# Seven products in place of eight in the second MLP layer of a streaming encoder, with the sums of weights on GpSimd

## The chip, the core and the metric

The kernel runs on one core of one Trainium2 chip. The metric is the device time of one execution in microseconds (us), lower is better. The engines are TensorE (PE, with its weight loads as PEld), VectorE (DVE), ScalarE (ACT), GpSimd (POOL) and SyncE (SP), which here issues all transfers.

## The reference, cut to what matters

One layer of a streaming encoder: a retention and convolution mixer, then an MLP with residuals and norms. The change lies in the MLP, for 2192 tokens, width 1024, inner width 4096, in float32:

```python
h = rms_norm(x, g_pre_mlp)
f = jnp.square(jax.nn.relu(h @ w_mlp_in)) @ w_mlp_out
x = x + rms_norm(f, g_post_mlp)
```

## The kernel before

**Precision.** Every float32 operand is split into a high part (a copy to the format fp32r, on ScalarE) and a low part (operand minus high part, on GpSimd: the residue). A product of two operands is three matmuls: high x high, high x low, low x high.

**Tiling.** Tokens are in six groups; the MLP takes them in three pairs (`FG`, index `G`), one after the other. The tokens of a pair are cut in two column halves `c` of 384, 384 and 320 columns (`NH2`). The inner width is walked in 16 blocks `b` of two 128-row tiles (`FB = 2`). For each block layer 1 makes four tiles (two rows by two column halves); layer 2 of the block before multiplies them by a 256 x 1024 slice of the second weight matrix and adds the result into eight output tiles for each half, `ya`, in SBUF.

**Layer 1** is done in seven products P1 to P7 in place of eight (a Strassen-Winograd scheme over two halves of the input width, two weight tiles and two column halves). Each product is 12 matmuls. Products accumulate in three PSUM banks `mm`; the partial sums are read out and combined by ScalarE and VectorE (`copy`, `added`), squared relu is taken in `out`, and `split` makes high and low parts `fh`, `fl`. In the first pair the sums of first-layer weights are made on GpSimd in `fetch_product` and kept in DRAM (`wprod`); the second and third pair load them.

**Layer 2** (`l2_tile`): for each output tile (`q`, `o`) and half `c` six matmuls go into one PSUM bank (`cv` or `aux` in turn) and one VectorE addition takes it into `ya`: 16 tiles in a block. Its weights come as four raw loads of 512 columns in a block; each is copied to the high part by ScalarE and gets its residue from GpSimd (`split_unit`).

**Order.** `plan` writes out the steps: after each product of layer 1 in block `b` come two or three tiles of layer 2 of block `b - 1`. `next_unit` fetches weights ahead, up to `WB - 2` = 7 slots out of `WB` = 9. Between the steps `tick` advances generators: in the first and the second pair, from block 2 on, `prologue` prepares the next pair (norms, residual, differences; it uses PSUM banks of `aux` as `pacc` and `sw`, additions and differences on GpSimd, and loads on SyncE's queue). The program order gives priorities; a planner with estimated costs fixes the final order on each engine before the run, so instructions of both layers are interleaved, and each engine then runs its own list in order.

Of the kernel before, what the change touches and what calls it, by code (L numbers as in the profile page):

```python
# [12 lines left out]
F32 = mybir.dt.float32  # L13
F32R = mybir.dt.float32r
# [67 lines left out]
P1, P2, P3, P4, P5, P6, P7 = range(7)  # L82
ORDER = (P1, P2, P6, P5, P7, P3, P4)
NG = 3
NH2 = [384, 384, 320]


def plan():


    for G in range(NG):
        for b in range(NFB):
            steps = []
# [3 lines left out]
            done = 0  # L97
            for n, x in enumerate(ORDER):
# [53 lines left out]
def build(nc, T):  # L152
    lg = _log_gamma()
    with tile.TileContext(nc, schedule_with_timeline_sim=True) as tc, ExitStack() as top:
# [6 lines left out]
        catp = ep(tc.tile_pool(name="catp", bufs=1))  # L161
        yop = ep(tc.tile_pool(name="yop", bufs=2))
        np_ = ep(tc.tile_pool(name="np_", bufs=2))
# [48 lines left out]
        for G, b, steps in plan():  # L212
            for what, x in steps:
                if what == "p":
                    units.append(("p", G, (b, x)))
                elif what == "w":
                    units.append(("l2", G, x))
        WB = 9
        rawps, RB = [], [5]
# [9 lines left out]
        def fetch(i):  # L229
# [10 lines left out]
            if kind == "p":  # L240
                return fetch_product(i, *units[i])
            hi = wpool.tile([P, 1024], F32R, tag="w", name="whi", bufs=WB)
            lo = wpool.tile([P, 1024], F32R, tag="w", name="wlo", bufs=WB)
# [25 lines left out]
        def fetch_product(i, _, G, bx):  # L269
# [31 lines left out]
            if NG > 1:  # L301
                keeping[i] = (wprod[b, x], op, None)

        unit_i = [0]

        def next_unit(kind, g, f):
# [846 lines left out]
        def layer1(G, b):  # L1153

            n = NH2[G]
            fh = [fp.tile([P, FB, NM], F32R, tag=f"fh{c}", name=f"fh{c}") for c in range(2)]
            fl = [fp.tile([P, FB, NM], F32R, tag=f"fl{c}", name=f"fl{c}") for c in range(2)]
            banks = {}
# [24 lines left out]
            def added(ps, t):  # L1183
                r = yop.tile([P, NM], F32, tag="yo", name="c", bufs=3)[:, :n]
                nc.vector.tensor_tensor(out=r, in0=ps, in1=t, op=ALU.add)
                return r

            def out(i, c, src, r=None):

                if r is None:  # L1190
                    r = yop.tile([P, NM], F32, tag="yo", name="r", bufs=3)[:, :n]
                    nc.scalar.activation(out=r, in_=src, func=AF.Relu)
                    nc.vector.scalar_tensor_tensor(out=r, in0=src, scalar=0.0, in1=r, op0=ALU.max, op1=ALU.mult)
                else:
                    nc.scalar.activation(out=r, in_=r, func=AF.Relu)
                    nc.scalar.activation(out=r, in_=r, func=AF.Square)
                split(r, fh[c][:, i, :n], fl[c][:, i, :n])

            def run():
                s1 = copy(product(P1, "y", True))  # L1200
                yield
                r = added(product(P2, "z", True), s1)
                out(0, 0, None, r)
                yield
# [5 lines left out]
                r = added(banks["w"], u3)  # L1210
                out(1, 1, None, r)
# [4 lines left out]
                out(1, 0, product(P4, "y", False))  # L1216
                yield

            return (fh, fl), run()

        def l2_tile(G, b, c, q, o, w, fhl, ya):
            whi, wlo = w
            fh, fl = fhl
            n = NH2[G]
            ps = mm_bank()[:, :n]
            mm3(ps, (lambda k: whi[:, (k * NO + o) * P:(k * NO + o + 1) * P],
                     lambda k: wlo[:, (k * NO + o) * P:(k * NO + o + 1) * P]),
                lambda k: fh[c][:, k, :n], lambda k: fl[c][:, k, :n], FB)
            y = ytile(ya, c, q * NO + o, n)
# [19 lines left out]
        def last_layer2(G, w, fhls, ya):  # L1249
# [5 lines left out]
            for c in range(2):  # L1255
                acc = np_.tile([P, WM], F32, tag="acc", name="acc")[:, :n]
                accs = [acc, st_tile()[:, :n]] if c else [acc]
                for q in range(FB):
                    for o in range(NO):
# [5 lines left out]
                                 lambda i: cols(w[i // FB * FB + q][1], i % FB)),  # L1265
                            lambda i: fhls[i // FB][0][c][:, i % FB, :n], lambda i: fhls[i // FB][1][c][:, i % FB, :n],
                            2 * FB)
# [21 lines left out]
        for G, b, steps in plan():  # L1289
# [7 lines left out]
            cur, run = layer1(G, b)  # L1297
            w = {}
            for what, x in steps:
# [3 lines left out]
                elif what == "w":  # L1303
                    w[x] = next_unit("l2", G, x)
                else:
                    q, o, c = x
# [70 lines left out]
```

## Time and profile before

| | |
|---|---|
| median of 3 runs | 2451.93 us (2447.64 to 2454.78) |
| profiled execution, its own time | 2451.31 us |
| its span, first to last instruction | 2449.4 us |
| TensorE busy | 2358.0 us (96%) |
| VectorE busy | 1512.6 us (62%) |
| ScalarE busy | 913.3 us (37%) |
| GpSimd busy | 1135.8 us (46%) |

The MLP's first pair runs from about 957 us to 1460 us, the second to about 1960 us, the third to the end. A busy share of TensorE counts overlapping matmuls once; how fast it works is read from the distance between the starts of matmuls.

### The profile page before, as it was taken

To read this page: it belongs to the slowest core of one execution; us is meant where nothing else is said; L and a number is where in the kernel's file an instruction comes from. 1 tells how busy PE (TensorE), PEld (TensorE's weight loads), DVE (VectorE), ACT (ScalarE), POOL (GpSimd) and SP (SyncE) were. 2 spreads that over 40 slices of the span, in tenths; PEclk is the share of its full clock that TensorE was granted. 3 is DMA by queue.
4 is the path that set the end of the run, shared out by engine and by line. 5 is a ranking of instruction groups with operands and counts; after the bars stand their busy time and mean duration, and the time that the engine had idled before them with its cause. 6 is when DMAs were issued, how large, how long until landed. Compare 5 with 4: busy or idle time off the path is not lost.

```text
span 2449.4 us, 40812 instructions
## 1 busy us (share of the span) xinstructions
PE 2358.0 (96%) x14538; PEld 2328.0 (95%) x14538; DVE 1512.6 (62%) x3320; ACT 913.3 (37%) x1928; POOL 1135.8 (46%) x1028
## 2 busy tenths in 40 slices
PE   7999999997999998899999999999999999999997
PEld 7898999997999998899999999999999999999996
DVE  8999896996987956456643347465433375333335
ACT  5544334133233234444444444333222353333332
POOL 6846232132132115778797785333522355332333
PEclk9999999998999999899999999999999999999998
DMA  8887787897687779658796567676854477555552
GB/s 312 294 312 274 258 293 253 253 346 255 202 299 256 251 238 351 217 204 306 268 325 206 185 226 234 233 232 225 287 168 148 157 235 252 181 175 187 179 183 86
DMA packets 246332, 584.53 MB, mean 239 GB/s; under 512 B 31984, under 2 KB 106480, under 8 KB 246128
## 3 DMA queue, kind: packets, MB, share of 16 engines
q1 hardware_dynamic: 246128, 581.92, 70.1%
q8 instruction: 115, 1.88, 0.3%
q14 instruction: 89, 0.73, 0.1%
HBM read 445.20 MB, written 136.61 MB: 238 GB/s over the span
## 4 chain that ended last, share of the span: by engine, by line
PE 71%; DVE 13%; DMA 9%; issue 3%; POOL 2%; ACT 1%; SPq 0%; DVEq 0%; POOLq 0%; ACTq 0%
PE mm L1171 8%; PE mm L1172 7%; PE mm L1173 7%; PE mm L459 5%; PE mm L461 5%; PE mm L460 5%; PE mma L459 4%; PE mma L460 4%; PE mma L461 4%; PE mmc L460 4%; PE mmc L461 4%; PE mmc L459 4%; DVE cv L780 4%; DMA s<-yscr 3%; PE mm L878 1%
## 5 line engine op out<-in xcount | busy, mean ns | idle before, releaser
L261 POOL TENSOR_TENSOR wlo<-raw,whi 128x512 fp32r<-128x512 f32 x276 | 362.7, 1334 | 283.1 <-PE mma L461 113.2
L1173 PE MATMUL mm<-op,wp 128*128 128x384 f32 (+1 forms) x1344 | 440.4, 329 | 4.6 <-POOL wp L300 4.5
L1172 PE MATMUL mm<-op,wp 128*128 128x384 f32 (+1 forms) x1344 | 441.7, 329 | 2.7 <-DVE op L329 2.7
L1171 PE MATMUL mm<-op,wp 128*128 128x384 f32 (+1 forms) x1344 | 438.9, 329 | 4.7 <-DMA wp<-wprod 2.3
L780 DVE SCALAR_TENSOR_TENSOR cv<-ext,par,cv 128x384 f32<-128x384 f32 (+1 forms) x720 | 381.4, 569 | 2.0
L459 PE MATMUL mm<-hhi,whi 128*128 128x384 f32 (+2 forms) x992 | 333.5, 336 | 18.5 <-ACT whi L260 7.0
L461 PE MATMUL mm<-hhi,wlo 128*128 128x384 f32 (+2 forms) x992 | 332.0, 336 | 5.9 <-DVE wlo L261 2.7
L460 PE MATMUL mm<-hlo,whi 128*128 128x384 f32 (+2 forms) x992 | 331.5, 335 | 0.3
L1233 DVE TENSOR_TENSOR ya<-mmc,ya 128x384 f32<-128x384 f32 (+1 forms) x344 | 182.3, 535 | 210.2 <-PE mmc L461 208.8
L1233 DVE TENSOR_TENSOR ya<-mma,ya 128x384 f32<-128x384 f32 (+1 forms) x344 | 182.8, 534 | 197.5 <-PE mma L461 196.7
L329 POOL TENSOR_TENSOR fl<-c,fh 128x384 fp32r<-128x384 f32 (+1 forms) x144 | 142.4, 989 | 335.8 <-ACT fh L328 306.2
L459 PE MATMUL mma<-fh,whi 128*128 128x384 f32 (+1 forms) x768 | 254.1, 332 | 6.9 <-DVE ya L1233 5.8
L1171 PEld LDWEIGHTS mm<-op,wp 128*128 128x128 f32 x1344 | 253.4, 189 | 7.7 <-DMA wp<-wprod 3.5
L1173 PEld LDWEIGHTS mm<-op,wp 128*128 128x128 f32 x1344 | 254.1, 189 | 5.4 <-POOL wp L300 5.2
L1172 PEld LDWEIGHTS mm<-op,wp 128*128 128x128 f32 x1344 | 254.1, 189 | 3.8 <-DVE op L329 3.3
L459 PE MATMUL mmc<-fh,whi 128*128 128x384 f32 (+1 forms) x768 | 251.1, 328 | 2.6 <-ACT fh L328 2.6
L460 PE MATMUL mma<-fl,whi 128*128 128x384 f32 (+1 forms) x768 | 251.7, 328 | 0.8 <-POOL fl L329 0.8
L460 PE MATMUL mmc<-fl,whi 128*128 128x384 f32 (+1 forms) x768 | 251.8, 328 | 0.6 <-POOL fl L329 0.6
L461 PE MATMUL mmc<-fh,wlo 128*128 128x384 f32 (+1 forms) x768 | 251.2, 328 | 1.0 <-POOL wlo L261 1.0
L461 PE MATMUL mma<-fh,wlo 128*128 128x384 f32 (+1 forms) x768 | 251.7, 328 | 0.4 <-POOL wlo L261 0.4
L260 ACT ACTIVATE whi<-raw 128x512 fp32r<-128x512 f32 x288 | 167.7, 623 | 153.0 <-PE mm L1173 83.1
L459 PEld LDWEIGHTS mm<-hhi,whi 128*128 128x128 f32 x992 | 191.8, 193 | 21.3 <-ACT whi L260 8.2
(234 smaller groups left out, 4872.2 us busy)
## 6 DMA issues: line engine op xcount, KB each, us to landing
wp<-wprod SPq DMA_DIRECT2D x224, 512.0 KB, 4.1
raw<-w SPq DMA_DIRECT2D x256, 256.0 KB, 3.8
wprod<-wp SPq DMA_DIRECT2D x112, 512.0 KB, 3.8
whi<-wkeep_in SPq DMA_DIRECT2D x108, 512.0 KB, 6.3
wlo<-wkeep_in SPq DMA_DIRECT2D x108, 512.0 KB, 5.4
raw<-w_in SPq DMA_DIRECT2D x72, 256.0 KB, 5.4
whi<-wkeep_out SPq DMA_DIRECT2D x36, 512.0 KB, 6.3
wlo<-wkeep_out SPq DMA_DIRECT2D x36, 512.0 KB, 5.6
```

The costliest lines, as they stand in the source:

```text
L260: nc.scalar.activation(out=hi[:, c], in_=raw, func=AF.Copy)
L261: (nc.vector if i < 24 and i % 4 == 0 else nc.gpsimd).tensor_tensor(out=lo[:, c], in0=raw, in1=hi[:, c].bitcast(F32), op=ALU.subtract)
L329: (eng or nc.gpsimd).tensor_tensor(out=lo, in0=src, in1=hi.bitcast(F32), op=ALU.subtract)
L459: nc.tensor.matmul(ps, whi(k), ahi(k), start=(k == 0), stop=False)
L460: nc.tensor.matmul(ps, whi(k), alo(k), start=False, stop=False)
L461: nc.tensor.matmul(ps, wlo(k), ahi(k), start=False, stop=(k == nk - 1))
L780: nc.vector.scalar_tensor_tensor(out=o, in0=src(t), scalar=wt, in1=o, op0=ALU.mult, op1=ALU.add)
L878: nc.tensor.matmul(o, hhi[:, k, c], whi, start=(k == 0), stop=False)
L1171: nc.tensor.matmul(ps, hi, ops[:, k, :n], start=start, stop=False, skip_group_check=not first)
L1172: nc.tensor.matmul(ps, hi, ops[:, 4 + k, :n], start=False, stop=False, skip_group_check=not first)
L1173: nc.tensor.matmul(ps, lo, ops[:, k, :n], start=False, stop=(k == 3), skip_group_check=not first)
L1233: last_y[0] = nc.vector.tensor_tensor(out=y, in0=ps, in1=y, op=ALU.add)
```

## The change

For blocks 2 to 13 of the second and the third pair (`SEVEN`), layer 2 is done by the same seven-product scheme over 2 x 2 pieces: two inner tiles, two column halves, and two halves of the output rows; `j` runs over two column pieces of 256 weights. A product is three matmuls on each of two output tiles (`l2_product`), 7 x 2 x 2 x 3 = 84 matmuls in a block. Each of the 28 results in a block is added into `ya` by VectorE; banks `y` (in `cv`), `w` and `z` (in `aux`) keep accumulating over several products between these reads. `layer1` makes seven operands in place of four, with four differences on VectorE (`diff`). `fetch_second` loads the same four raw weights, makes the four sums for each `j` on GpSimd, and splits 14 pieces of 256 columns, two to a weight slot. `SHARE` says how many of the 14 products stand after each product of layer 1. Operands `fo` are one tile with high and low part, nine buffers, in all blocks. The pool `yop` has a default of three buffers, though its tiles name three themselves.

```diff
+ORDER2 = (P1, P5, P6, P3, P7, P2, P4)
+SHARE = (2, 4, 6, 7, 9, 11, 14)
+SEVEN = range(2, NFB - 2)
...
+            if G and b - 1 in SEVEN:
+                seven = [(j, x) for j in range(2) for x in ORDER2]
+                for n, x in enumerate(ORDER):
+                    steps.append(("p", x))
+                    while done < SHARE[n]:
+                        if done % 2 == 0:
+                            steps.append(("q", (b - 1, done // 2)))
+                        steps.append(("u", (done, *seven[done])))
+                        done += 1
...
-        yop = ep(tc.tile_pool(name="yop", bufs=2))
+        yop = ep(tc.tile_pool(name="yop", bufs=3))
...
+        def fetch_second(i, _, G, bt):
+            b, t = bt
+            op = wpool.tile([P, 1024], F32R, tag="w", name="wq", bufs=WB)
+            ready[i] = op
+            if t == 0:
+                raws2[G, b] = [[rawps[-1].tile([P, 512], F32, tag="raw", name="raw2", bufs=RB[-1]) for _ in range(2)]
+                               for _ in range(2)]
+                for r in range(2):
+                    for q in range(2):
+                        nc.sync.dma_start(raws2[G, b][r][q], T["w2"][b * FB + r][:, q * 512:(q + 1) * 512])
+            H = 256
+            tt = nc.gpsimd.tensor_tensor
+            for s in (2 * t, 2 * t + 1):
+                j, x = s // 7, ORDER2[s % 7]
+                (a11, a12), (a21, a22) = [[q[:, j * H:(j + 1) * H] for q in r] for r in raws2[G, b]]
+                if x == P5:
+                    t2 = x1p.tile([P, 2 * H], F32, tag="sum", name="s34", bufs=1)
+                    sums[G, b, j] = s3, s4 = t2[:, :H], t2[:, H:]
+                    tt(out=s3, in0=a11, in1=a21, op=ALU.subtract)
+                    tt(out=a21, in0=a21, in1=a22, op=ALU.add)
+                    tt(out=a11, in0=a21, in1=a11, op=ALU.subtract)
+                    tt(out=s4, in0=a12, in1=a11, op=ALU.subtract)
...
+                o = (s % 2) * 2 * H
+                nc.scalar.activation(out=op[:, o:o + H], in_=src, func=AF.Copy)
+                nc.gpsimd.tensor_tensor(out=op[:, o + H:o + 2 * H], in0=src, in1=op[:, o:o + H].bitcast(F32),
+                                        op=ALU.subtract)
...
-                room -= 1 if units[i + n][0] == "p" else 2
+                room -= 1 if units[i + n][0] in "pq" else 2
...
+            def operand(key, r):
+                t = fo[key] = fp.tile([P, 2, NM], F32R, tag="fo", name="fo", bufs=9)
+                split(r, t[:, 0, :n], t[:, 1, :n])
...
+            def diff(out, a, b):
+                nc.vector.tensor_tensor(out=out, in0=a, in1=b, op=ALU.subtract)
+                return out
...
                 r = added(product(P3, "w", False), u2)
-                out(0, 1, None, r)
+                b12 = out(0, 1, None, r)
+                if seven:
+                    t1 = diff(b11, b12, b11)
+                    operand(P5, t1)
+                    t2 = diff(x1p.tile([P, NM], F32, tag="t2", name="t2", bufs=2)[:, :n], b22, t1)
+                    operand(P6, t2)
+                    operand(P7, diff(b12, b22, b12))
+                yield
+                b21 = out(1, 0, product(P4, "y", False))
+                if seven:
+                    operand(P2, b21)
+                    operand(P4, diff(t2, b21, t2))
...
+        def l2_product(G, b, s, j, x, w, fo, ya, ybanks):
+            n = NH2[G]
+            base = s % 2 * 512
+            for a in range(2):
+                o = 2 * j + a
+                if x == P1:
+                    ybanks["y", a] = cvp.tile([P, 512], F32, tag="cv", name="l2y")
+                if x in (P5, P2):
+                    ybanks["w" if x == P5 else "z", a] = auxp.tile([P, 512], F32, tag="aux", name="l2w")
+                ps = ybanks[{P5: "w", P3: "w", P2: "z"}.get(x, "y"), a][:, :n]
...
+                nc.tensor.matmul(ps, hi, fh, start=first, stop=False, skip_group_check=not first)
+                nc.tensor.matmul(ps, hi, fl, start=False, stop=False, skip_group_check=not first)
+                nc.tensor.matmul(ps, lo, fh, start=False, stop=True, skip_group_check=not first)
+                r, c = {P1: (0, 0), P2: (0, 0), P6: (0, 1), P3: (0, 1), P7: (1, 1), P5: (1, 1), P4: (1, 0)}[x]
+                y = ytile(ya, c, 4 * r + o, n)
+                last_y[0] = nc.vector.tensor_tensor(out=y, in0=ps, in1=y, op=ALU.add)
```

## Rows read from the trace of the kernel before

**Rows 1.** The page, busy us of each engine over the span.

```profile
PE 2358.0 (96%) x14538; PEld 2328.0 (95%) x14538; DVE 1512.6 (62%) x3320; ACT 913.3 (37%) x1928; POOL 1135.8 (46%) x1028
```

**Rows 2.** Windows, calm stretches of the second and third pair, busy us by engine.

```profile
core 0: us, PE busy (x) PEld busy (x) DVE busy (x) ACT busy (x) POOL busy (x), PEclk, DMA share, GB/s
1700.00:1850.00 150.00, 148.62 (x854) 147.49 (x853) 62.17 (x122) 42.96 (x86) 60.13 (x58) 1.00 0.67 222
...
2100.00:2300.00 200.00, 200.00 (x1366) 200.00 (x1365) 73.06 (x153) 63.91 (x136) 64.13 (x60) 1.00 0.55 181
```

**Rows 3.** Waits of TensorE, second pair (1460 to 1960 us).

```profile
PE mm L1171 <- DMA wp<-wprod: 2.3, 3, 0.9
PE mma L459 <- DVE ya L1233: 1.8, 2, 1.2
...
PE mma L459 <- DVE ya L1231: 0.2, 1, 0.2
```

**Rows 4.** Timeline of TensorE, one stretch of the second pair, one of the third.

```profile
1609.75 0.34 PE L1172 MATMUL mm<-op,wp 128*128 128x384 f32 x1
...
1620.85 0.34 PE L461 MATMUL mmc<-fh,wlo 128*128 128x384 f32 x1
...
2129.47 0.31 PE L1173 MATMUL mm<-op,wp 128*128 128x320 f32 x1
...
2139.88 0.31 PE L460 MATMUL mma<-fl,whi 128*128 128x320 f32 x1
```

**Rows 5.** Timeline of GpSimd, instructions back to back: start us, us.

```profile
1346.02 1.01 POOL L329 TENSOR_TENSOR fl<-r,fh 128x384 fp32r<-128x384 f32 x1
1347.00 2.56 POOL L261 TENSOR_TENSOR wlo<-raw,whi 128x512 fp32r<-128x512 f32 x2
...
1690.37 1.43 POOL L529 TENSOR_TENSOR s<-s 128x256 f32<-128x256 f32 x2 [1.22 <-DVE s L527]
1691.75 1.01 POOL L329 TENSOR_TENSOR fl<-c,fh 128x384 fp32r<-128x384 f32 x1
...
2147.48 0.88 POOL L329 TENSOR_TENSOR fl<-c,fh 128x320 fp32r<-128x320 f32 x1 [5.81 <-ACT fh L328]
2148.32 2.57 POOL L261 TENSOR_TENSOR wlo<-raw,whi 128x512 fp32r<-128x512 f32 x2
```

**Rows 6.** Line 567, VectorE, two SBUF inputs: duration ns min/median/max.

```profile
L567 DVE TENSOR_TENSOR s<-st,s x12: 557/1190/1652, 936.9 to 991.4; 128x384 f32<-128x384 f32 x12
```

**Rows 7.** Windows of 31 us in the first pair, columns as in rows 2.

```profile
1177.00:1208.00 31.00, 27.00 (x142) 26.68 (x141) 13.27 (x26) 12.93 (x29) 25.26 (x23) 0.89 0.82 283
1208.00:1239.00 31.00, 31.00 (x179) 30.73 (x178) 22.37 (x40) 13.31 (x26) 25.13 (x21) 1.00 0.86 285
1239.00:1270.00 31.00, 31.00 (x181) 31.00 (x180) 10.88 (x20) 13.81 (x26) 30.21 (x28) 1.00 0.93 337
...
1332.00:1363.00 31.00, 31.00 (x180) 31.00 (x180) 10.73 (x21) 12.98 (x26) 22.84 (x20) 1.00 0.54 187
```

**Rows 8.** Groups by line and shape: busy us, mean ns, idle before.

```profile
L1233 DVE TENSOR_TENSOR ya<-mmc,ya 128x384 f32<-128x384 f32 x240 | 132.3, 554 | 140.9 <-PE mmc L461 140.2
...
L1233 DVE TENSOR_TENSOR ya<-mma,ya 128x320 f32<-128x320 f32 x104 | 50.9, 489 | 91.2 <-PE mma L461 91.2
...
L260 ACT ACTIVATE whi<-raw 128x512 fp32r<-128x512 f32 x288 | 167.7, 623 | 153.0 <-PE mm L1173 83.1
```

**Rows 9.** The page, transfers: count, size, median us to landing.

```profile
wp<-wprod SPq DMA_DIRECT2D x224, 512.0 KB, 4.1
```

**Rows 10.** Timeline of VectorE, then TensorE, around 1190 us.

```profile
1193.09 0.61 DVE L527 SCALAR_TENSOR_TENSOR s<-s,par,sw 128x384 f32<-128x384 f32 x1 [3.07 <-DMA s<-yscr]
...
1194.23 0.69 PE L459 MATMUL mma<-fh,whi 128*128 128x384 f32 x1 [4.00 <-DVE ya L1233]
```

**Rows 11.** Window just behind that wait, columns as in rows 2.

```profile
1194.00:1198.00 4.00, 3.77 (x12) 3.77 (x13) 2.28 (x5) 0.00 (x0) 4.00 (x4) 0.50 0.92 341
```

**Rows 12.** Waits of VectorE, second pair (1545 to 1770 us): total, times, longest.

```profile
DVE s L527 <- DMA s<-yscr: 8.8, 5, 2.8
```

**Rows 13.** Waits of GpSimd, first pair (960 to 1460 us).

```profile
POOL wp L300 <- ACT wp L299: 39.7, 20, 3.9
```

More of the change, by code (lines that the diff above doesn't have):

```diff
@@ L97, in plan @@
             done = 0
+            if G and b - 1 in SEVEN:
[7 more added lines that the diff above has]
+                        done += 1
+                yield G, b, steps
+                continue
             for n, x in enumerate(ORDER):
@@ L217, in build @@
                     units.append(("l2", G, x))
+                elif what == "q":
+                    units.append(("q", G, x))
         WB = 9
@@ L241, in fetch @@
                 return fetch_product(i, *units[i])
+            if kind == "q":
+                return fetch_second(i, *units[i])
             hi = wpool.tile([P, 1024], F32R, tag="w", name="whi", bufs=WB)
@@ L302, in fetch_product @@
                 keeping[i] = (wprod[b, x], op, None)
+        raws2 = {}
+        def fetch_second(i, _, G, bt):
[20 more added lines that the diff above has]
+                    tt(out=s4, in0=a12, in1=a11, op=ALU.subtract)
+                src = {P1: lambda: a11, P2: lambda: a12, P3: lambda: sums[G, b, j][1], P4: lambda: a22,
+                       P5: lambda: a21, P6: lambda: a11, P7: lambda: sums[G, b, j][0]}[x]()
+                o = (s % 2) * 2 * H
+                nc.scalar.activation(out=op[:, o:o + H], in_=src, func=AF.Copy)
+                nc.gpsimd.tensor_tensor(out=op[:, o + H:o + 2 * H], in0=src, in1=op[:, o:o + H].bitcast(F32),
+                                        op=ALU.subtract)
         unit_i = [0]
@@ L1155, in layer1 @@
             n = NH2[G]
-            fh = [fp.tile([P, FB, NM], F32R, tag=f"fh{c}", name=f"fh{c}") for c in range(2)]
-            fl = [fp.tile([P, FB, NM], F32R, tag=f"fl{c}", name=f"fl{c}") for c in range(2)]
+            seven = G > 0 and b in SEVEN
+            fo = {}
             banks = {}
@@ L1196, in out @@
                     nc.scalar.activation(out=r, in_=r, func=AF.Square)
-                split(r, fh[c][:, i, :n], fl[c][:, i, :n])
+                if not seven:
+                    operand((i, c), r)
+                return r
+            def diff(out, a, b):
+                nc.vector.tensor_tensor(out=out, in0=a, in1=b, op=ALU.subtract)
+                return out
             def run():
@@ L1202, in run @@
                 r = added(product(P2, "z", True), s1)
-                out(0, 0, None, r)
+                b11 = out(0, 0, None, r)
+                if seven:
+                    operand(P1, b11)
                 yield
@@ L1210, in run @@
                 r = added(banks["w"], u3)
-                out(1, 1, None, r)
+                b22 = out(1, 1, None, r)
+                if seven:
+                    operand(P3, b22)
                 yield
                 r = added(product(P3, "w", False), u2)
-                out(0, 1, None, r)
+                b12 = out(0, 1, None, r)
+                if seven:
+                    t1 = diff(b11, b12, b11)
[3 more added lines that the diff above has]
+                    operand(P7, diff(b12, b22, b12))
                 yield
-                out(1, 0, product(P4, "y", False))
+                b21 = out(1, 0, product(P4, "y", False))
+                if seven:
+                    operand(P2, b21)
+                    operand(P4, diff(t2, b21, t2))
                 yield
-            return (fh, fl), run()
+            return fo, run()
+        def l2_product(G, b, s, j, x, w, fo, ya, ybanks):
[8 more added lines that the diff above has]
+                ps = ybanks[{P5: "w", P3: "w", P2: "z"}.get(x, "y"), a][:, :n]
+                hi, lo = (w[:, base + i * 256 + a * P:base + i * 256 + (a + 1) * P] for i in range(2))
+                first = x in (P1, P2, P5)
+                fh, fl = fo[x][:, 0, :n], fo[x][:, 1, :n]
+                nc.tensor.matmul(ps, hi, fh, start=first, stop=False, skip_group_check=not first)
[4 more added lines that the diff above has]
+                last_y[0] = nc.vector.tensor_tensor(out=y, in0=ps, in1=y, op=ALU.add)
         def l2_tile(G, b, c, q, o, w, fhl, ya):
             whi, wlo = w
-            fh, fl = fhl
             n = NH2[G]
@@ L1227, in l2_tile @@
                      lambda k: wlo[:, (k * NO + o) * P:(k * NO + o + 1) * P]),
-                lambda k: fh[c][:, k, :n], lambda k: fl[c][:, k, :n], FB)
+                lambda k: fhl[k, c][:, 0, :n], lambda k: fhl[k, c][:, 1, :n], FB)
             y = ytile(ya, c, q * NO + o, n)
@@ L1265, in last_layer2 @@
                                  lambda i: cols(w[i // FB * FB + q][1], i % FB)),
-                            lambda i: fhls[i // FB][0][c][:, i % FB, :n], lambda i: fhls[i // FB][1][c][:, i % FB, :n],
+                            lambda i: fhls[i // FB][i % FB, c][:, 0, :n], lambda i: fhls[i // FB][i % FB, c][:, 1, :n],
                             2 * FB)
@@ L1297, in build @@
             cur, run = layer1(G, b)
-            w = {}
+            w, ybanks = {}, {}
             for what, x in steps:
@@ L1304, in build @@
                     w[x] = next_unit("l2", G, x)
+                elif what == "q":
+                    wq = next_unit("q", G, x)
+                elif what == "u":
+                    l2_product(G, b - 1, *x, wq, prev, ya, ybanks)
+                    tick()
                 else:
```

## The prediction

> **What bounds the kernel now.** I read the views from the coarse to the fine. The table of busy time comes first [rows 1]: TensorE is busy in 96% of the span, VectorE in 62%, GpSimd in 46%, ScalarE in 37%. Shares over the whole span mix stages, so next comes the view by windows, in the stage that the change touches [rows 2]. In a calm stretch of the second pair (1700 to 1850 us) TensorE is busy for 148.62 of 150 us, in one of the third pair (2100 to 2300) for 200.00 of 200, at a granted clock of 1.00 (2.4 GHz). GpSimd has 60.13 of 150 and 64.13 of 200 there. The list of what TensorE waited for in the second pair has six entries, from 2.3 to 0.2 us, together 6.8 us in 500; the two longest are 2.3 us for product weights and 1.8 us for VectorE's additions [rows 3]. So in these two stages the end is set by the number of matmuls times the step from one to the next, and by nothing else.
>
> That step I take from the timeline, not from the means: a matmul's row lasts 0.34 us because neighbours overlap. In the second pair 65 starts without a hole lie between 1609.75 and 1620.85 us, so one step is 11.10 / 64 = 0.1734 us for 384 columns. In the third, 72 starts from 2129.47 to 2139.88 give 10.41 / 71 = 0.1466 us for 320 columns [rows 4].
>
> **What the change removes.** One block of layer 2 is 16 tiles of 6 matmuls = 96 before. After, it is 7 products on two pieces j of the output rows, with two output tiles in each and 3 matmuls for a tile: 7 x 2 x 2 x 3 = 84. Layer 1 keeps 84 in both. 12 blocks of each pair are changed, so 144 matmuls go from each: 144 x 0.1734 = 25.0 us and 144 x 0.1466 = 21.1 us, together **46.1 us**. A block shrinks from 180 to 168 matmuls: 31.2 to 29.1 us in the second pair, 26.4 to 24.6 in the third. The other three engines must fit into these shorter blocks.
>
> **GpSimd, the engine to fear.** The trace of before has no sums of layer-2 weights; their like are 256-column subtractions elsewhere. Two of these back to back take 1.38 us to the next start, 0.69 each; a 384-column one takes 0.98, a 320-column one 0.84, and two of 512 columns 2.56 together [rows 5]. A block of before costs GpSimd 4 weight residues of 512 columns (5.1 us) and 4 operand residues (3.9 or 3.4): 9.0 or 8.5 us. After: 14 weight residues and 8 sums, all of 256 columns, 22 x 0.69 = 15.2 us, and 7 operand residues, 6.9 or 5.9 us. That makes 22.1 of 29.1 us (76%) and 21.1 of 24.6 (86%). In the second pair the preparation of the third adds 32 instructions in some eight blocks, at most 32 x 0.98 / 8 = 3.9 us in a block.
>
> VectorE's four new differences in a block take both inputs from SBUF. The rows for such an instruction of 384 columns run from 0.557 to 1.652 us [rows 6], so it is held up by as much as 1.1 us, about one GpSimd instruction. If GpSimd in turn loses 0.55 us to each, that is 2.2 us more, and a block needs 28.2 of 29.1 us with the preparation, 23.3 of 24.6 in the third pair. Full, but under the block. Does a GpSimd that full stop TensorE? The first pair answers: it makes its weight sums on GpSimd now, and in the window 1239 to 1270 us GpSimd is busy for 30.21 of 31 us while TensorE has 31.00 of 31; in 1332 to 1363 it has 22.84 beside 31.00 [rows 7]. I therefore cost the weight sums at nothing. The cover is the margin of 0.9 and 1.3 us in a block and the weights' being fetched seven units ahead, half a block. If it is gone, operands are late, first those of P5, which layer 2 needs second in the next block.
>
> The Trainium skill speaks against this edit: its GPSIMD Engine Reference (section 4.1, engine selection) sends elementwise work on tiles to VectorE and calls GpSimd about twice slower with two inputs. By that rule the time would be that of rival 1; the rows agree with the ratio (0.98 against 0.55 us [rows 5, 8]), but a slower engine off the chain costs nothing by itself. The Trainium skill's page SBUF — State Buffer (SBUF: two separate sides) says that GpSimd and a VectorE instruction with two SBUF inputs lock each other out for a whole instruction; the spread in [rows 6] agrees with it.
>
> **VectorE.** Additions into the result rise from 16 to 28 in a block, of 0.554 or 0.489 us [rows 8], so 12 x 0.55 = 6.6 us more, and the four differences at 0.55 to 1.65 us add 2.2 to 6.6 [rows 6]. At the upper ends a block holds 28 x 0.55 + 4 x 0.55 + 6.6 = 24.2 of 29.1 us; the third pair 28 x 0.49 + 4 x 0.49 + 6.6 = 22.3 of 24.6. It fits, but its order matters, because the products now accumulate on banks that VectorE reads in between: P6 may not start on bank y before P1's sum is read. In the written order a layer-1 product of 12 matmuls (2.1 us) lies in most of these gaps. The one short gap is P7 to P4 of the second half: three tiles, 9 x 0.1734 = 1.56 us. What must fit is a matmul's 0.34, an addition's 0.55 and, when a difference stands ahead, up to 1.65 us: 2.54, so 0 to 0.98 us can show in a block, 0 to 23.5 us in 24 blocks. Matmuls of the next layer-1 product can be scheduled into it, as the interleaved order now shows they are, so I take 0.1 us a block, **2.4 us**, near the lower end.
>
> **ScalarE, transfers, buffers.** ScalarE copies 14 pieces of 256 columns instead of 4 of 512 (0.623 us each [rows 8]); even at that price for each it is 6 us more, against 42.96 us busy in 150 now [rows 2]. Three more operand splits are 1.6 us. Nothing of it is on the path, with more than half of the block free as cover. The layer-2 weights are still four loads in a block. The nine weight slots turn over faster: 14 tiles go through them in a block instead of 11, so a slot's lead of six units falls from about 17 us to 6/14 x 29.1 = 12.5 us, against 4.1 us to land [rows 9]; nothing, unless the queue itself stands. The output pool's new default count changes nothing, as all its tiles name their own three buffers; finer operand tiles in the unchanged blocks are free too.
>
> **What I add for the preparation.** In the first pair, under the same kind of preparation, VectorE sat 3.07 us at a normalisation that waited for a transfer [rows 10], and the addition behind it released a bank to TensorE after 4.00 us. TensorE's clock then fell to 0.50 (1.2 GHz) for 1194 to 1198 us [rows 11], and the window of 31 us has 142 matmuls where the next has 179 [rows 7]: 37 x 0.1734 = **6.4 us**. The second pair has the same preparation, and with banks shared between pacc, sw and the new w and z it has less slack. VectorE already waits 8.8 us for such loads there [rows 12]. Bounds: nothing (the full window of [rows 7]) to three such events, 19 us. I take one, 6.4 us.
>
> **The sum**, against the profiled execution's 2451.3 us (2449.4 span and 1.9 around it; the median of the runs is 0.6 higher): 2451.3 - 46.1 + 2.4 + 6.4 = **2414 us**.
>
> **Rivals.** (1) GpSimd becomes the bound after all. For it: in the first pair it also sits idle for ScalarE's copies, 39.7 us in 20 waits, over sixteen blocks 2.5 us each [rows 13]; a 28.2 or 23.3 us load and 2.5 us of such waits is 30.7 and 25.8 us. Over the block by 1.6 us in eight blocks and by 1.2 in twelve: 27 us given back on top of the forecast's terms, 2441 us; with half of it 2428. Against it: 30.21 of 31 us without a TensorE wait. Chance 0.24, 2425 to 2444. (2) All of the gain is eaten, or TensorE was not the bound there: 2444 to 2459. Speaks against it: 200.00 of 200. Chance 0.10. (3) Slower: the wait of 1190 us returns as a habit, VectorE's queue holding up a bank in every second block, each with the fall of the clock: 12 x 6.4 = 77 us, 2451 - 46 + 77 = 2482 us. It decides from (46.1 + 7.4) / 24 = 2.2 us lost in a block. For it: the bank chains, and differences that last up to 1.65 us. Against: one such wait in sixteen blocks of the first pair. Chance 0.12.
>
> **How the numbers follow.** The forecast has 0.54 (2402 to 2425: 46.1 us and the few waits of now gone at the low end, the upper bounds of half the short gaps at the high one). A measurement of this kernel tells 0.3%, 7.4 us, from no change, so faster is below 2444.6: 0.54 + 0.24 = 0.78; same 0.10; slower 0.12. The range 2402 to 2446 takes in the forecast and rival 1.
>
> **What will show it.** Right: 144 fewer matmuls a pair; TensorE still 29 of 29 us in windows of the third pair after 2040; GpSimd at 75 to 97% there, with VectorE's differences at 0.55 to 1.65 us each. GpSimd at 100% beside TensorE's waits for operand or weight residues would show rival 1; waits for the additions with clocks below 1.00, rival 3. The prediction is wrong if pair lengths shrink by much less than 25 and 21 us.

## The result, and the profile after

The changed kernel takes 2411.81 us (median of four runs, 2409.09 to 2417.93) against 2453.36 (four runs, 2447.64 to 2455.14): a ratio of 0.9835, 95% interval 0.9822 to 0.9848, so 37 to 44 us faster. The forecast was 2414. Its total came out right, though two steps that it priced at nothing came to some ten microseconds each, in opposite directions.

The page's busy time of the changed kernel, the line that answers to [rows 1]:

```profile
PE 2312.4 (96%) x14250; PEld 2277.5 (95%) x14250; DVE 1708.5 (71%) x3704; ACT 1005.1 (42%) x2240; POOL 1470.6 (61%) x1532
```

The 288 matmuls are gone (14538 to 14250 records). GpSimd carries 504 instructions more, VectorE 384 and ScalarE 312; TensorE still has 96%. The share hides where the time went, so I cut the span at the first layer-1 product of each pair, read from the timelines of both profiled executions:

| us | before | after | difference | the forecast's matmuls |
|---|---|---|---|---|
| up to the first pair | 957.1 | 960.7 | +3.6 | 0 |
| first pair | 514.6 | 499.9 | -14.7 | 0 |
| second pair | 513.3 | 497.1 | -16.1 | -25.0 |
| third pair to the end | 464.4 | 449.5 | -14.9 | -21.1 |

The two changed pairs give 31.0 of the 46.1 us; the first pair, whose matmuls are the same, gives another 14.7. Across the change and the nine kernels below that share its first pair's code and its nine weight slots and do layer 2 by seven products later on, that pair lasts 499.7 to 506.9 us, so a single profile tells it to some 4 us (their mean is 502.9, and the change lies at the low end), and the +3.6 is no more than that.

Windows of the changed kernel with the columns of [rows 2] (us, then busy time and records of PE, PEld, DVE, ACT and POOL, the granted clock, DMA share, GB/s). The first two lie in the second pair beside the preparation, the third behind it, the rest in the third pair:

```profile
1719.00:1748.00 29.00, 25.55 (x146) 24.93 (x145) 22.30 (x42) 9.50 (x24) 25.46 (x32) 1.00 0.78 265
1748.00:1777.00 29.00, 26.83 (x145) 26.11 (x144) 23.30 (x33) 10.69 (x25) 25.83 (x32) 0.94 0.82 262
1806.00:1835.00 29.00, 29.00 (x169) 29.00 (x168) 19.90 (x37) 13.35 (x32) 22.81 (x29) 1.00 0.50 161
2038.00:2067.00 29.00, 29.00 (x200) 29.00 (x199) 17.16 (x35) 13.30 (x33) 22.42 (x29) 1.00 0.48 156
2183.00:2212.00 29.00, 28.67 (x194) 28.14 (x192) 20.27 (x43) 13.07 (x35) 24.96 (x33) 1.00 0.60 196
2100.00:2300.00 200.00, 196.53 (x1324) 193.90 (x1323) 130.39 (x282) 94.94 (x244) 173.96 (x229) 1.00 0.56 187
```

GpSimd sits at 25.5 and 25.8 of 29 us beside the preparation and at 87% in the third pair (173.96 of 200; the forecast had 86 to 95%). The full windows exist, 29.00 of 29, but between 2100 and 2300 us TensorE now has 1324 matmuls where [rows 2] have 1366. Its waits say why. Those of the changed kernel's second pair (1460 to 1935 us), with us in total, times and the longest:

```profile
PE mm L1227 <- DMA wp<-wprod: 7.9, 8, 1.5
PE l2w L1315 <- DVE ya L1320: 2.5, 2, 1.9
PE l2y L1315 <- DVE ya L1320: 2.2, 1, 2.2
PE l2y L1315 <- ACT wq L355: 0.6, 1, 0.6
```

and those from 1935 us to the end:

```profile
PE mm L1227 <- DMA wp<-wprod: 4.8, 10, 1.0
PE mma L514 <- DVE ya L1183: 0.5, 1, 0.5
```

The wait for product weights was 2.3 us in the second pair of before [rows 3]. It is now the longest in total in both pairs, and it is the one that the forecast priced at nothing. No line names GpSimd.

What a distance between two starts of matmuls has beyond the step of [rows 4] is called a hole here. Adding up the holes, in the third pair up to 2345 us here and below, gives in the second pair 12.1 us before and 22.8 after, in the third 2.2 and 10.5. In front of layer 1's products they rise from 4.2 to 11.1 and from 1.3 to 8.2 (together +13.8), in front of layer 2 from 7.8 to 11.7 and from 0.9 to 2.2 (+5.2).

The limit of 2345 us leaves out the end of the third pair. Behind its last product of layer 1, where the last block of layer 2 runs alone, before has 4.4 us of holes and the change 0.2. The waits of TensorE in before from 2404 us to the end; the change has none there:

```profile
PE mmc L459 <- ACT fh L328: 0.9, 1, 0.9
PE mmc L460 <- POOL fl L329: 0.6, 1, 0.6
PE mma L461 <- POOL wlo L261: 0.4, 1, 0.4
```

So over the whole third pair the holes rise by some 4 us and not by 8.

The lead of a product load, from its issue to the first matmul that reads it, has a median of 17.0 and 15.5 us in blocks 4 to 13 of the two pairs before, and of 5.9 and 5.0 us after; 1 and 0 of 70 were under 4.5 us, now 11 and 28 are. One such load of the third pair, in the chain of waits (start, us) and in TensorE's timeline of the changed kernel:

```profile
2207.99 4.79 DMA wp<-wprod
```

```profile
2212.83 0.42 PE L1227 MATMUL mm<-op,wp 128*128 128x320 f32 x1 [0.90 <-DMA wp<-wprod]
```

The load lands 4.79 us after its issue, the matmul is ready 0.90 us earlier. With a lead of 15 us nobody would have seen it.

### The profile page after: what moved, and what is told of

The parts are those of the page before. It is cut to its first block, busy times and chain, and to the rows that moved or that the text cites. A ratio compares the mean times of both kernels' runs of the same rounds, so it can differ in the third digit from the quotient of the medians.

```text
span 2407.3 us, 41425 instructions
## 1 busy us (share of the span) xinstructions
PE 2312.4 (96%) x14250; PEld 2277.5 (95%) x14250; DVE 1708.5 (71%) x3704; ACT 1005.1 (42%) x2240; POOL 1470.6 (61%) x1532
## 5 line engine op out<-in xcount | busy, mean ns | idle before, releaser
L1227 PE MATMUL mm<-op,wp 128*128 128x384 f32 (+1 forms) x1344 | 441.9, 329 | 13.3 <-DMA wp<-wprod 12.7
L283 POOL TENSOR_TENSOR wlo<-raw,whi 128x512 fp32r<-128x512 f32 x180 | 239.0, 1347 | 127.2 <-ACT whi L282 52.2
L1320 DVE TENSOR_TENSOR ya<-l2y,ya 128x384 f32<-128x384 f32 (+1 forms) x384 | 194.6, 519 | 117.1 <-PE l2y L1317 116.3
L356 POOL TENSOR_TENSOR wq<-raw,wq 128x256 fp32r<-128x256 f32 x240 | 183.1, 776 | 58.7 <-ACT wq L355 58.0
L384 POOL TENSOR_TENSOR fo<-c,fo 128x384 fp32r<-128x384 f32 (+1 forms) x168 | 166.2, 990 | 65.3 <-ACT fo L383 64.1
L516 PEld LDWEIGHTS mm<-hhi,wlo 128*128 128x128 f32 x992 | 190.7, 193 | 10.2 <-DMA wlo<-wkeep_in 3.8
L515 PEld LDWEIGHTS mm<-hlo,whi 128*128 128x128 f32 x992 | 191.0, 193 | 1.5 <-DVE hlo L732 1.1
L1320 DVE TENSOR_TENSOR ya<-l2w,ya 128x384 f32<-128x384 f32 (+1 forms) x288 | 143.1, 517 | 19.3 <-PE l2w L1317 16.7
L1241 DVE TENSOR_TENSOR c<-mm,sn 128x384 f32<-128x384 f32 (+1 forms) x144 | 76.5, 532 | 112.7 <-PE mm L1229 74.5
L322 POOL TENSOR_TENSOR wp<-raw,wp 128x512 fp32r<-128x512 f32 x96 | 126.9, 1327 | 43.9 <-ACT wp L321 31.5
L282 ACT ACTIVATE whi<-raw 128x512 fp32r<-128x512 f32 x192 | 112.9, 623 | 85.4 <-DMA raw<-w_in 19.0
```

The source lines that it names most:

```text
L283: (nc.vector if i < 24 and i % 4 == 0 else nc.gpsimd).tensor_tensor(out=lo[:, c], in0=raw, in1=hi[:, c].bitcast(F32), op=ALU.subtract)
L322: tt(out=op[:, H:], in0=src, in1=op[:, :H].bitcast(F32), op=ALU.subtract)
L356: nc.gpsimd.tensor_tensor(out=op[:, o + H:o + 2 * H], in0=src, in1=op[:, o:o + H].bitcast(F32), op=ALU.subtract)
L384: (eng or nc.gpsimd).tensor_tensor(out=lo, in0=src, in1=hi.bitcast(F32), op=ALU.subtract)
L515: nc.tensor.matmul(ps, whi(k), alo(k), start=False, stop=False)
L516: nc.tensor.matmul(ps, wlo(k), ahi(k), start=False, stop=(k == nk - 1))
```

## The experiments

Four questions: what the seven products give by themselves; whether GpSimd's sums cost anything; why the lead fell; and where the first pair's gain comes from. The first theory was the forecast's (the matmuls saved, GpSimd off the path), with rival 1, GpSimd as the bound, against it.

**Operand tiles alone.** All of the change except the seven products.

```diff
-SEVEN = range(2, NFB - 2)
+SEVEN = range(0)
```

> The changed kernel with no block done by seven products in layer 2: only the operand tiles (one tile for high and low part, nine buffers) stay of the change. In the changed kernel the first pair, which has no new products, became 14.7 us shorter while the mixer before it took 3.6 us more. Theory A: that is the work of the operand tiles, so this kernel is about 11 us faster than before, 2441 us, with a first pair of about 500 us. Rival: the tiles are free and the first pair's gain came with the seven products, so this kernel takes as long as before, 2452 us, with a first pair of about 514 us.

Measured: 2447.43 us, ratio 0.9962 (0.9946 to 0.9978), so some 9 us faster than before without one matmul less. The pairs last 504.5, 516.5 and 462.7 us: the gain is in the first. The seven products by themselves give 0.9835 / 0.9962, 1.27% or 31 us, the same 31.0 us as in the table of the pairs.

**The third pair alone.**

```diff
-            if G and b - 1 in SEVEN:
+            if G == 2 and b - 1 in SEVEN:
...
-            seven = G > 0 and b in SEVEN
+            seven = G == 2 and b in SEVEN
```

> Seven products in the third pair alone. If the gains of the pairs stand each for itself, the second pair goes back by the 16.1 us that it gained: 2428 us, with the third pair to the end at about 449.5 us and the second at 513. If the pairs hang together (one pair's buffers or loads holding up the next), one of the two lengths differs by more than 4 us.

Measured: 2428.67 us, 0.9895 (0.9872 to 0.9917), with 501.5, 508.3 and 448.4 us. The third pair is as short as in the full change: it needs nothing of the second, and what it lacks to 21.1 us it lacks by itself.

**GpSimd without the sums.** This kernel leaves out the four sums for each `j` and takes unsummed weights in their place; the matmuls are those of the change.

```diff
-                    t2 = x1p.tile([P, 2 * H], F32, tag="sum", name="s34", bufs=1)
-                    sums[G, b, j] = s3, s4 = t2[:, :H], t2[:, H:]
-                    tt(out=s3, in0=a11, in1=a21, op=ALU.subtract)
-                    tt(out=a21, in0=a21, in1=a22, op=ALU.add)
-                    tt(out=a11, in0=a21, in1=a11, op=ALU.subtract)
-                    tt(out=s4, in0=a12, in1=a11, op=ALU.subtract)
+                    sums[G, b, j] = a22, a12
```

> The four sums of layer-2 weights for each piece are left out (the products take unsummed weights), so GpSimd has 8 instructions of 0.69 us less in a block, 5.5 us of 24.6 or 29.1; the matmuls are the same. Theory A (GpSimd is off the path, the 15 us that the changed pairs lack come from late loads of product weights and from the preparation): no more than 4 us faster than the changed kernel, 2408 to 2412. Rival (GpSimd's fill makes the shortfall): most of the 15 us comes back, 2397 to 2400.

Measured: 2418.15 us, 0.9859 (0.9838 to 0.9881), no faster than the changed kernel. Second pair 497.1, third 451.3 us; the holes in front of layer 1 are 9.4 and 11.0 us. Eight instructions less in a block on the engine that is fullest beside TensorE bring nothing: GpSimd is not the bound, and rival 1 falls.

**More on GpSimd**: the four differences too.

```diff
-                nc.vector.tensor_tensor(out=out, in0=a, in1=b, op=ALU.subtract)
+                nc.gpsimd.tensor_tensor(out=out, in0=a, in1=b, op=ALU.subtract)
```

> The four differences of a block move from VectorE to GpSimd. GpSimd then needs about 30 of 29.1 us in the second pair's blocks with preparation, 26 in its others, and 24.5 of 24.6 us in the third pair. Theory A (room was left on GpSimd): 5 to 12 us slower than the changed kernel, about 2420, mostly in the second pair. Rival 1 (GpSimd was the bound already): every block grows by the 3.4 to 3.9 us, 24 blocks, about 2495. Rival 2 (VectorE's differences, locked out by GpSimd, make the shortfall): faster, about 2402.

Measured: 2439.43 us, 0.994 (0.9919 to 0.996); 503.0, 508.9 and 458.5 us. The third pair's window in this kernel:

```profile
2110.00:2310.00 200.00, 194.53 (x1294) 189.69 (x1293) 108.65 (x250) 91.98 (x239) 188.06 (x252) 1.00 0.49 174
```

GpSimd goes to 94% and TensorE loses 30 of 1324 matmuls. From 1974 to 2400 us its longest wait in total is now for layer-2 pieces that ScalarE copies too late:

```profile
PE l2w L1315 <- ACT wq L355: 5.9, 9, 0.7
```

So rival 1 was wrong about the place and right that it is near: four instructions in a block further GpSimd does cost time, 0.994 - 0.9835 of 2453, about 25 us, though less than their own length (4 x 0.98 or 0.84 us [rows 5] in 24 blocks, 87 us). Unlike the sums, these four stand between layer 1's results and layer 2's operands, so the run doesn't tell a fuller GpSimd from operands that come later.

**The lead: three edits without effect.** The second theory was that product loads stand behind the layer-2 raw loads in the transfer queue; next, that they are asked for too late; then, that the nine slots are too few for 14 tiles in a block, as the forecast's 12.5 us had it. One edit each: the raw loads of the next block issued early, one unit more fetched ahead, and one slot less (with it the fetch reaches one unit less far).

```diff
-            if t == 0:
+            for e in ([b] if t == 0 else [b + 1] if t == 3 and b + 1 in SEVEN else []):
+                if (G, e) in raws2:
+                    continue
...
```

> In the changed kernel TensorE's gaps before products of layer 1 grew from 4.2 to 11.1 us in the second pair and from 1.3 to 8.2 in the third, most of them ended by a load of product weights. SyncE's queue runs in order, and raw loads of layer-2 weights stand in it waiting for GpSimd (23 waits, up to 4.0 us, in the third pair). Here the four raw loads of a block are issued half a block earlier, at the fourth weight slot of the block before. Theory A (loads of product weights queue behind the raw loads): those gaps fall to 6 us together and the kernel gains about 10 us, ratio to before 0.979. Rival (nine slots for 14 tiles a block are too few, whatever the order): gaps and time stay, ratio 0.983.

```diff
-            room, n = WB - 2, 0
+            room, n = WB - 2 + (g > 0 and kind in ("p", "q", "l2")), 0
```

> In the second and third pair weights are fetched eight units ahead instead of seven, with the same nine slots. If the fetch order gives the lead (the term that the prediction put at nothing: 6/14 of a block, 12.5 us), the gaps before layer-1 products shrink by a third, 6 us faster, ratio 0.981. If the slots give it, since a load is issued as soon as its slot is free, nothing changes: 0.983.

```diff
-        WB = 9
+        WB = 8
```

> Eight weight slots in place of nine, and the fetch one unit shorter, in the whole kernel; read by the lengths of the pairs, since the mixer changes too. Theory A (slots set the lead of the product loads): the lead falls to about the landing time, the gaps before layer-1 products in the second and third pair double to about 40 us, and each of the two pairs takes about 10 us more than the changed kernel's 497 and 449.5. Rival (the gaps come from the order, not from slots): the two pairs stay within 4 us.

| | median us | ratio (95%) | second, third pair us | holes before layer 1, us |
|---|---|---|---|---|
| the change | 2411.81 | 0.9835 (0.9822 to 0.9848) | 497.1, 449.5 | 11.1, 8.2 |
| raw loads early | 2416.92 | 0.9859 (0.984 to 0.9878) | 497.0, 448.6 | 10.8, 7.0 |
| one unit further ahead | 2413.78 | 0.9836 (0.9818 to 0.9854) | 501.4, 448.4 | 10.3, 7.6 |
| one slot less | 2414.51 | 0.9845 (0.9815 to 0.9875) | 498.9, 449.8 | 12.9, 8.7 |

None moves the time. The first two edits hardly reached the chip, though. In both traces TensorE, VectorE and GpSimd run their instructions in the order of the change, and the weight loads of the two pairs, raw and product, are issued in the same order too; the raw loads of the third pair stand within 1.8 us of where they stood. So the raw loads did not go out half a block early, and the theory that product loads stand behind them was not tested by that run. What it shows is how far one and the same order scatters: 2411.81, 2413.78 and 2416.92 us. Asking one unit earlier gave the planner nothing that it could use, so the depth of the fetch isn't the limit. Eight slots did change the order. The lead stays at 5.8 and 5.1 us with one unit more, and at 5.5 and 5.1 with eight slots. What does shrink with the slot is another distance: a layer-2 piece is copied into its slot 21.9 and 19.3 us before its first matmul in the change, and 18.4 and 15.5 us with eight. So taking a slot away shortens the stay of the layer-2 pieces and not the lead of the product loads.

**The lead: who takes the freed slot.** Last theory: a freed slot goes first to a layer-2 piece, made ready 20 us early, and the product load takes what is left. Here each copy of such a piece is ordered behind the latest addition into the result that the program has written down by then. This is an order on the planner only, and the matmuls and copies are the same.

```diff
-                nc.scalar.activation(out=op[:, o:o + H], in_=src, func=AF.Copy)
+                hi = nc.scalar.activation(out=op[:, o:o + H], in_=src, func=AF.Copy)
+                if last_y[0] is not None:
+                    tc.add_manual_dep(hi.ins, last_y[0].ins.name, mybir.DependencyInfo(
+                        mybir.DependencyClass.NoSync, mybir.DependencyReason.DATA))
```

> In the changed kernel the load of a product's weights is issued 5.0 us (median, third pair) before TensorE uses them, against 15.5 before the change, and it takes 3.4 us to land; the layer-2 pieces are copied into their slots 19.3 us before use. Here each copy of a layer-2 piece is placed, in the planner's order, behind the latest addition into the result that the program has reached, which is seven units ahead of its use: about 12 us. No wait is added on the chip and no work changes. Theory A (layer-2 pieces, made ready too early, hold the nine slots, so product loads start late): the lead of product loads rises to 10 us or more, the gaps before layer-1 products fall from 19 us together to about 6, and the kernel gains 8 to 13 us, ratio to before 0.979. Rival (nine slots are too few for 14 tiles anyway): the gaps move to the layer-2 products and the time stays, 0.983.

Measured: 2418.98 us, 0.9864 (0.984 to 0.9887); 503.0, 508.3 and 445.5 us. In the third pair it does what the theory says: pieces are copied 7.8 us ahead, the lead of product loads rises from 5.0 to 8.7 us, none of 70 is under 4.5, and the holes in front of layer 1 go from 8.2 to 0.7 us. Its waits of TensorE there (2040 to 2345 us), all that are left, and its window:

```profile
PE l2y L1318 <- DVE ya L1323: 0.5, 1, 0.5
```

```profile
2100.00:2300.00 200.00, 199.17 (x1341) 196.44 (x1340) 133.51 (x288) 96.18 (x248) 176.87 (x233) 1.00 0.56 189
```

Its 445.5 us are below every kernel that has the change's third pair without this order (448.4 to 452.2). Of the 7.5 us of holes that go, some 4 come off the time: in front of layer 2 the holes rise from 2.2 to 5.9 us, as the rival expected, though only by half. The same run speaks against the theory of the raw loads, which the early issue had left untested. SyncE now stands longer for a raw buffer, and the product loads are earlier all the same. Its waits from 2040 to 2345 us, in the change and here:

```profile
SPq L338 <- POOL wq L356: 25.8, 24, 4.0
```

```profile
SPq L338 <- POOL wq L359: 86.2, 39, 7.8
```

In the second pair the same order does harm (holes of 33.5 us in place of 22.8): beside the preparation 9.0 us of waits for product weights stay, and VectorE's additions come late as well. So it was put in the third pair alone (against the kernel just shown):

```diff
-                if last_y[0] is not None:
+                if G == 2:
```

> The layer-2 pieces are held back in the planner's order in the third pair alone. There the hold raised the lead of product loads from 5.0 to 8.7 us and took the gaps before layer-1 products from 8.2 to 0.7 us and the third pair from 449.5 to 445.5; in the second pair, beside the preparation, it cost 11 us. If the pairs stand each for itself: second pair about 497, third about 445.5, 4 us faster than the changed kernel, ratio to before 0.982. Rival (the hold in the third pair only looked good because its start was shifted by the second): third pair near 449.5, ratio 0.983.

Measured: 2414.11 us, 0.9831 (0.9804 to 0.9858); 499.7, 500.1 and 446.7 us. The third pair is 2.8 us shorter than in the change, with no wait of TensorE left from 2040 to 2345 us, a lead of 8.9 us and holes of 1.6 in front of layer 1. As a whole it can't be told from the change: 2.8 us is 0.1%, and the second pair, whose orders are the change's, is 3.0 us longer in this profile.

**Two more tries.** The preparation of the third pair stepped more seldom in the second, and block 1 done by seven products too.

```diff
-                slow[0] = 2
+                slow[0] = 2 + G
```

> In the second pair the preparation of the third advances at every third step instead of every second; its work is the same. The second pair has 10.9 us of gaps before layer-2 products there, ended by VectorE's additions, which the prediction priced at 6.4 us. If they come from VectorE's and the banks' load by the preparation being too dense, they halve: 4 to 6 us faster, ratio 0.981, second pair about 492 us. If they come from single waits in VectorE's queue for loads, the same waits stand elsewhere: same time, 0.983.

```diff
-SEVEN = range(2, NFB - 2)
+SEVEN = range(1, NFB - 2)
```

> Seven products also in block 1 of the second and third pair. By the count of matmuls 12 x (0.1734 + 0.1466) = 3.8 us less, ratio 0.982. GpSimd and SyncE are busy with the epilogue of the pair before in those blocks: if they set the pace there, no gain or a loss of up to 5 us, 0.985.

Stepping more seldom: 2421.01 us, 0.9865 (0.9845 to 0.9885), second pair 502.5 us with holes of 15.8 us in front of layer 1 and 13.3 in front of layer 2. A miss: neither kind of hole falls. One block more in each pair: 2424.08 us, 0.9881 (0.9862 to 0.99), 504.3 and 455.4 us, with holes of 18.1 and 14.3 in front of layer 1. The 24 matmuls saved (3.8 us at the steps of [rows 4]) are lost several times over. Most of these holes end with a product load, and they lie all along both pairs (in the third from 2020 to 2353 us) and not only at block 1; why one block more brings them is open.

**The ninth operand buffer.** The tiles alone once more, with eight buffers, the count that the two sets of four gave before.

```diff
-                t = fo[key] = fp.tile([P, 2, NM], F32R, tag="fo", name="fo", bufs=9)
+                t = fo[key] = fp.tile([P, 2, NM], F32R, tag="fo", name="fo", bufs=8)
```

> The operand tiles alone, as in the kernel without seven products, with eight buffers in place of nine, which is as much as the kernel before has in its four tags. In that kernel block 1 of the first pair takes 30.5 us against 40.6 before. Theory A (finer tiles, high and low part together, change the planner's order of GpSimd's work there): block 1 stays near 30.5 us. Rival (the ninth buffer): it goes back to about 40 us and the first pair to 514.

Measured: 2451.59 us, 0.9995 (0.9983 to 1.0007): the gain is gone, the first pair lasts 517.5 us. TensorE's waits from 957 to 1005 us, in before, in this kernel and in the change:

```profile
PE mm L1173 <- POOL wp L300: 4.5, 1, 4.5
PE mm L1172 <- DVE op L329: 2.7, 2, 1.9
PE mm L1171 <- ACT op L328: 1.1, 1, 1.1
```

```profile
PE mm L1229 <- POOL wp L322: 5.9, 2, 4.5
PE mm L1228 <- DVE op L384: 2.2, 2, 1.4
PE mm L1227 <- ACT op L383: 1.5, 1, 1.5
```

```profile
PE mm L1229 <- POOL wp L322: 1.5, 1, 1.5
```

With eight buffers block 1 of the first pair lasts 40.6 us (before) and 41.1 (this kernel), with nine 30.5 (the change, and the tiles alone). In the windows of before this block also has TensorE's clock below full:

```profile
977.00:987.00 10.00, 4.35 (x16) 3.59 (x17) 9.38 (x8) 3.88 (x8) 10.00 (x8) 0.72 0.92 345
987.00:997.00 10.00, 6.93 (x25) 6.11 (x24) 7.01 (x6) 3.40 (x7) 8.43 (x7) 0.67 0.86 284
```

and the corresponding stretch of the change has 45 matmuls in ten microseconds where those have 16 and 25:

```profile
980.00:990.00 10.00, 8.33 (x45) 7.47 (x44) 7.93 (x7) 6.38 (x14) 10.00 (x8) 1.00 0.92 327
```

The kernel with eight buffers has 16 and 24 matmuls and a clock of 0.76 and 0.67 from 979 to 999 us, like before. So it is the ninth buffer, not the finer tile, that shortens the first pair: by waits of some 7 us and by the clock that fell behind them.

## Why the prediction was right, and where it was not

**Right: what was the bound.** Matmuls times the step was the end in both pairs: the records fell by 288 and, behind the preparation, TensorE has 29.00 of 29 us in a block of 168. The seven products alone are worth 31 us, so rival 2 (all eaten) is out, and rival 3 too: in windows of 10 us from 1470 to 2340 the clock is below 1.00 only between 1750 and 1770 (0.94 and 0.89), one event and not a habit.

**Right: GpSimd.** The sum in a block was near (87% in the third pair against 86 to 95), and leaving the sums out brings nothing. That they cost nothing was shown; that the margin was as thin as the forecast had it is argued, from the four differences more that cost about 25 us. By the Trainium skill's rule of engine selection (GPSIMD Engine Reference, section 4.1) the differences belong on VectorE, and there the run agrees; for the sums, off the path, it costs nothing to break it.

**Wrong: "nothing, unless the queue itself stands".** The weight slots' lead was priced at zero from an even share of nine slots (6/14 of a block, 12.5 us against 4.1 us to land). The same share had fitted the second pair of before (17 us, measured 17.0). Measured in the change: 5.9 and 5.0 us, and 13.8 us more of holes in front of layer 1's products. The error was to share the slots evenly. They are handed on in the planned order, which holds layer-2 pieces some 20 us and leaves the remainder to the loads of products, which go straight into their slot. In the third pair this is shown: with the pieces held back the holes in front of layer 1 are gone, in two kernels, while the number of slots and the depth of fetching had no effect. In the second pair it is not: there the same order made the holes longer, and why the product loads stay late beside the preparation is open.

**Too high: the short gap and the preparation, 2.4 + 6.4 us.** Holes in front of layer 2 rose by 5.2 us (to 2345 us). The short gap's mechanism was there, differences ahead of the additions that release a bank, but its upper end of 1.65 us was too low for a single instruction (below). The preparation's was not the named one. The forecast had a normalisation that waits for a transfer; in front of the two longest of these holes (2.1 and 2.3 us, at 1738.9 and 1758.0 us) the additions stood behind differences. The one fall of the clock that the term allowed for came behind the second.

**Wrong: "finer operand tiles in the unchanged blocks are free too".** The tiles are; the ninth buffer is not, it gives about 8 us (0.9962 with it, 0.9995 without, of 2453). The step looked at the tiles' size and passed over their number, nine in place of eight. Why one buffer more makes just the order of block 1 better was not settled.

**The sum.** -46.1, then +13.8 and +5.2 of holes, -4.2 for those at the end of the third pair that only before has, and -11.1 outside the two pairs make -42.4; the profiles differ by 42.1 (2449.4 to 2407.3). The forecast's -37.3 met this by luck in part: a cost of 13.8 us and gains of 11.1 and 4.2, all left out, nearly cancel. The total is right, its working only for the matmuls and GpSimd. The kernels with the tiles alone keep 2.9 us of the holes at the end, so most of that 4.2 came with the seven products; why was not tried.

## What to carry to other kernels

When tiles of two kinds share one ring of slots, work out the lead of each from how long the other holds a slot, not from an even share, and compare the smaller one with the time to land. A change that comes with one buffer more should be run once with that buffer alone, since here it was worth a fifth of the whole gain. Here an engine filled to 87% off the path cost nothing, and four more instructions in a block, on the way to layer 2's operands, cost about 25 us.

## What the runs showed of the hardware

The differences on VectorE, line 1262, in the second pair of the changed kernel (duration in ns, min/median/max), against 557/1190/1652 in [rows 6]:

```profile
L1262 DVE TENSOR_TENSOR c<-c x24: 544/1096/3386, 1553.8 to 1887.9; 128x384 f32<-128x384 f32 x24
L1262 DVE TENSOR_TENSOR t<-c x12: 541/630/1220, 1555.3 to 1887.4; 128x384 f32<-128x384 f32 x12
L1262 DVE TENSOR_TENSOR t<-r,t x12: 544/1070/6048, 1560.7 to 1899.2; 128x384 f32<-128x384 f32 x12
```

The medians are as forecast, the longest is not. The timeline of the changed kernel around the one of 6.05 us, all engines, cut to VectorE and GpSimd and the matmul that waited:

```profile
1751.35 0.74 POOL L349 TENSOR_TENSOR raw<-raw,raw 128x256 f32<-128x256 f32 x1
1751.43 6.05 DVE L1262 TENSOR_TENSOR t<-r,t 128x384 f32<-128x384 f32 x1 [0.63 <-POOL fo L384]
...
1752.04 1.02 POOL L384 TENSOR_TENSOR fo<-c,fo 128x384 fp32r<-128x384 f32 x1
...
1753.01 1.02 POOL L384 TENSOR_TENSOR fo<-r,fo 128x384 fp32r<-128x384 f32 x1
...
1753.98 1.44 POOL L356 TENSOR_TENSOR wq<-raw,wq 128x256 fp32r<-128x256 f32 x2
...
1755.38 0.86 POOL L661 TENSOR_TENSOR s<-st,s 128x320 f32<-128x320 f32 x1
...
1756.20 0.86 POOL L661 TENSOR_TENSOR s<-st 128x320 f32<-128x320 f32 x1
...
1757.40 0.55 DVE L1320 TENSOR_TENSOR ya<-l2y,ya 128x384 f32<-128x384 f32 x1
...
1758.00 0.44 PE L1315 MATMUL l2y<-fo,wq 128*128 128x384 f32 x1 [2.17 <-DVE ya L1320]
```

GpSimd runs seven instructions without a hole from 1751.35 to 1757.06 us, and the difference, begun 0.08 us behind the first, ends 0.42 us after the last. The addition behind it releases a bank, and TensorE stands for 2.17 us. I had bounded such an instruction by one GpSimd instruction; here a row of seven without a hole between them held it for the whole row. It is one case: of the 48 differences in these rows the next longest took 3.39 us. The Trainium skill (SBUF — State Buffer, SBUF: two separate sides) says that whichever of the two starts first has the shared ports for its whole instruction; this timeline agrees that the difference was shut out, and shows that its turn needn't come at the next instruction. That the ports are the cause here is argued from the rows, not tried by itself.
